# Log-sum-exp of 16384 rows: a range check moved ahead of the last rows, and two bulk loads issued as four transfers each

## The chip, the cores and the metric

The kernel runs on one core of a Trainium2 chip. The metric is device time in microseconds (us) of one execution. Engines: DVE is VectorE, ACT is ScalarE, PE is TensorE, POOL is GpSimd, SP is the engine whose queue issues the loads and the store. "Landing" of a DMA is the moment at which the sixteenth of its sixteen semaphore increments arrives (the trace of the kernel before holds 288 of them for its 18 DMAs).

## The reference

```python
x: float32 [32, 512, 1024]          # np.random.randn
max_x = np.max(x, axis=-1, keepdims=True)
return max_x.squeeze(-1) + np.log(np.sum(np.exp(x - max_x), axis=-1))
```

## The kernel before

The 16384 rows are laid out as 128 partitions with 128 rows (columns of `sumexp`) each. The kernel bets that no row needs its maximum subtracted: it sums exp(x) directly, takes the log, stores the result, and then checks whether every sum lay within a safe range. Only if the check fails does a slow fallback run and overwrite the result. Loads go into a ring of 48 row slots. In the list below `R8` is eight rows whose exp ACT makes and DVE reduces, `T` rows are summed by DVE in another form, and `A` rows by ACT itself.

```python
RING = 48
loads = ["R8 R8", "R8 R8", "R8 R8", "R7 R6 A A", "R6 R5 A A A", "R5 R4 A", "R5 R4", "R5 T3",
         "R3 A A A", "R3 A", "R2 T2", "R3", "R1 A", "T2", "T1", "A", "A"]      # 17 loads, 128 rows
...
def load(p0, c0, size):
    return nc.sync.dma_start(out=ring[:, p0 : p0 + size, :], in_=x_rows[:, c0 : c0 + size, :])
...
    nc.scalar.activation(out=res[:, EARLY:NC], in_=sumexp[:, EARLY:NC], func=AF.Ln)
    nc.sync.dma_start(out=out_view, in_=res)                        # the 18th DMA
    # range check of columns 0..126: clamp, then count what the clamp changed
    nc.vector.tensor_scalar(out=clamped[:, 0:LAST], in0=sumexp[:, 0:LAST], scalar1=LOW, scalar2=HIGH, ...)
    nc.vector.scalar_tensor_tensor(out=clamped[:, 0:LAST], ..., op1=ALU.not_equal, accum_out=bad[:, 0:1])
    nc.tensor.matmul(count, lhsT=bad[:, 0:1], rhs=far, start=True, stop=False)
    # the last row: enough that one of its first 64 inputs is not tiny, and that its sum is not huge
    nc.vector.reduce_max(out=bad[:, 2:3], in_=last_row[:, 0, 0 : d // 16], axis=AX.X)
    nc.vector.tensor_scalar(out=bad[:, 1:2], in0=bad[:, 2:3], scalar1=LOG_LOW, op0=ALU.is_lt, ...)
    nc.tensor.matmul(count, lhsT=bad[:, 1:2], rhs=far, start=False, stop=False)
    nc.tensor.matmul(count, lhsT=sumexp[:, LAST:NC], rhs=ones, start=False, stop=True)
    nc.vector.tensor_scalar(out=fine, in0=count, scalar1=HIGH, op0=ALU.is_lt, ...)
    all_fine = nc.values_load(fine[0:1, 0:1], engines=[ACT, DVE], ...)   # a register on ACT and on DVE
    with tc.If(all_fine < 1):
        ...                                                          # the fallback
```

The framework places all semaphores. DMAs take eight semaphores in rotation (102, 103 and 105 to 110). At the end of the program SP waits for twelve semaphores in a fixed order (105, 106, 103, 107, 102, 108, 113, 109, 112, 110, 101, 104); then SP, ACT, DVE and PE each report with a closing drain, POOL collects the reports (at 162.47 us in the kernel before), and a second closing round follows (POOL has its reports at 162.95).

Of the kernel before, what the change touches and what calls it, by code (L numbers as in the profile page):

```python
# [9 lines left out]
LOW, HIGH = 1e-15, 1e15  # L10
LOG_LOW = -34.0
# [3 lines left out]
def kernel(  # L15
# [5 lines left out]
    nc = tc.nc  # L21
    P = nc.NUM_PARTITIONS
    fp32 = mybir.dt.float32
    i32 = mybir.dt.int32
    AF = mybir.ActivationFunctionType
    AX = mybir.AxisListType
    ALU = mybir.AluOpType

    x_flat = x.flatten_outer_dims()
    n, d = x_flat.shape  # L30
# [4 lines left out]
    x_rows = x_flat.rearrange("(p c) d -> p c d", p=P)  # L35
# [6 lines left out]
    loads = [  # L42
        "R8 R8", "R8 R8", "R8 R8", "R7 R6 A A", "R6 R5 A A A", "R5 R4 A", "R5 R4", "R5 T3",
        "R3 A A A", "R3 A", "R2 T2", "R3", "R1 A", "T2", "T1", "A", "A",
    ]
    loads = [[(op[0], int(op[1:] or 1)) for op in load.split()] for load in loads]
    assert sum(s for ops in loads for _, s in ops) == NC
    ENGINES = [mybir.EngineType.Activation, mybir.EngineType.DVE]
    EARLY = 104
    LAST = NC - 1  # L50

    big = ctx.enter_context(tc.tile_pool(name="big", bufs=1))
    stats = ctx.enter_context(tc.tile_pool(name="stats", bufs=1))
    psum = ctx.enter_context(tc.tile_pool(name="psum", bufs=1, space=bass.MemoryType.PSUM))

    ring = big.tile([P, RING, d], fp32, name="ring")
    sumexp = stats.tile([P, NC], fp32, name="sumexp")
    res = stats.tile([P, NC], fp32, name="res")
    clamped = stats.tile([P, NC], fp32, name="clamped")
    bad = stats.tile([P, 3], fp32, name="bad")  # L60
    fine = stats.tile([1, 1], i32, name="fine")
    far = stats.tile([P, 1], fp32, name="far")
    ones = stats.tile([P, 1], fp32, name="ones")
    last_exp = psum.tile([P, 1, d], fp32, name="last_exp")
    count = psum.tile([1, 1], fp32, name="count")
# [3 lines left out]
    nc.vector.memset(far, 100 * HIGH)  # L69

    def load(p0, c0, size):
        return nc.sync.dma_start(out=ring[:, p0 : p0 + size, :], in_=x_rows[:, c0 : c0 + size, :])  # L72

    def without_wait(ins, group, reason):

        tc.declare_no_dep(ins.ins, group=group, reason=reason)

    c = 0
    p = 0
    for ops in loads:  # L80
        size = sum(s for _, s in ops)
        if p + size > RING:
            p = 0
        dma = load(p, c, size).ins
        for how, s in ops:
            v = ring[:, p : p + s, :]
            sums = sumexp[:, c : c + s]
            if how == "A":
                o = v if c < LAST else last_exp
                exp = nc.scalar.activation(out=o, in_=v, func=AF.Exp, accum_out=sums)  # L90
            else:
                exp = nc.scalar.activation(out=v, in_=v, func=AF.Exp)  # L92
            without_wait(exp, "loads", "the slot's earlier users came before this load")
            without_wait(exp, "exps", "the slot's earlier users came before this load")
            without_wait(exp, "sums", "the slot's earlier users came before this load")
            tc.add_to_no_dep_group("exps", exp.ins)
            added = []
            if how == "R":
                added = [nc.vector.reduce_sum(out=sums, in_=v, axis=AX.X)]  # L99
            elif how == "T":  # L100
                for r in range(s):
                    lo = ring[:, p + r, 0:H]
                    added.append(
                        nc.vector.scalar_tensor_tensor(  # L104
                            out=lo, in0=lo, scalar=1.0, in1=ring[:, p + r, H:d],
                            op0=ALU.mult, op1=ALU.add, accum_out=sums[:, r : r + 1],
                        )
                    )
            for add in added:
                tc.declare_no_dep(add.ins, dma, reason="ScalarE has waited for it")  # L110
                without_wait(add, "loads", "they came before this one")
            for add in added:
                tc.add_to_no_dep_group("sums", add.ins)
            c += s
            p += s
            last_row = v
        tc.add_to_no_dep_group("loads", dma)
        if c == EARLY + 14:
            nc.scalar.activation(out=res[:, 0:EARLY], in_=sumexp[:, 0:EARLY], func=AF.Ln)  # L119

    nc.scalar.activation(out=res[:, EARLY:NC], in_=sumexp[:, EARLY:NC], func=AF.Ln)  # L121
    nc.sync.dma_start(out=out_view, in_=res)




    nc.vector.tensor_scalar(  # L127
        out=clamped[:, 0:LAST], in0=sumexp[:, 0:LAST],
        scalar1=LOW, scalar2=HIGH, op0=ALU.max, op1=ALU.min,
    )  # L130
    nc.vector.scalar_tensor_tensor(  # L131
        out=clamped[:, 0:LAST], in0=clamped[:, 0:LAST], scalar=0.0, in1=sumexp[:, 0:LAST],
        op0=ALU.bypass, op1=ALU.not_equal, accum_out=bad[:, 0:1],
    )
    nc.tensor.matmul(count, lhsT=bad[:, 0:1], rhs=far, start=True, stop=False)  # L135
    nc.vector.reduce_max(out=bad[:, 2:3], in_=last_row[:, 0, 0 : d // 16], axis=AX.X)  # L136
    nc.vector.tensor_scalar(  # L137
        out=bad[:, 1:2], in0=bad[:, 2:3], scalar1=LOG_LOW, scalar2=None, op0=ALU.is_lt
    )
    nc.tensor.matmul(count, lhsT=bad[:, 1:2], rhs=far, start=False, stop=False)  # L140
    nc.tensor.matmul(count, lhsT=sumexp[:, LAST:NC], rhs=ones, start=False, stop=True)  # L141

    nc.vector.tensor_scalar(out=fine, in0=count, scalar1=HIGH, scalar2=None, op0=ALU.is_lt)  # L143
    all_fine = nc.values_load(
        fine[0:1, 0:1], engines=ENGINES, min_val=0, max_val=1,
# [2 lines left out]
    with tc.If(all_fine < 1, preferred_fallthrough_block=False):  # L148
        with tc.tile_critical(sync_engine=mybir.EngineType.Activation):
            with nc.semaphore("landed") as landed, nc.semaphore("ready") as ready:  # L150
                rows = 0
                steps = 0
                for c0 in range(0, NC, RING):
# [3 lines left out]
                    if c0:  # L157
# [5 lines left out]
                        out=neg, in_=v, op=ALU.max, axis=AX.X, negate=True  # L163
# [3 lines left out]
                        out=v, in0=v, in1=neg[:, :, None].to_broadcast([P, s, d])  # L167
# [5 lines left out]
                        out=sumexp[:, c0 : c0 + s], in_=v, axis=AX.X  # L173
# [39 lines left out]
```

## Time and profile before

| | before |
|---|---|
| median (6 runs) | 165.12 us (164.97 to 165.41) |
| traced execution | 164.92 us, span 163.1 us |
| last row lands | 159.01 us |
| store issued, landed | 160.46, 162.01 us |
| SP's and DVE's first closing drain begin | 162.37 and 162.38 us |
| end, counted from the last landing | 4.13 us |

From the page of the kernel before: engine busy time, the data rate in 40 slices, and the DMA queue.

```profile
PE 0.4 (0%) x6; PEld 0.2 (0%) x6; DVE 122.0 (75%) x44; ACT 116.8 (72%) x53; POOL 0.2 (0%) x4
GB/s 257 514 321 450 514 370 402 514 418 354 514 418 354 514 438 407 377 482 482 450 394 422 436 420 402 402 450 434 434 418 442 422 440 400 426 423 421 409 314 18
q1 hardware_dynamic: 2592, 67.18, 95.9%
```

The transfers fill the 16 DMA engines for 95.9% of the span, while DVE (75% busy) and ACT (72%) have slack. The load is the bound. A change that adds no bandwidth can touch only the 1.7 us before the first packet and the last 4 us: what happens after the last row has landed at 159.01.

The timeline of that tail (start, duration, engine, line, operation, output<-input, shapes):

```profile
159.03 1.02 ACT L90 ACTIVATE last_exp<-ring 128x1024 f32<-128x1024 f32 x1
159.29 0.08 DVE L104 DVE_READ_ACCUMULATOR ring<-ring 128x1 f32 x1
159.48 0.23 DVE L127 TENSOR_SCALAR clamped<-sumexp 128x127 f32<-128x127 f32 x1
159.74 0.29 DVE L131 SCALAR_TENSOR_TENSOR clamped<-clamped,sumexp 128x127 f32<-128x127 f32 x1
...
159.96 0.21 DVE L136 TENSOR_REDUCE bad<-ring 128x1 f32<-128x64 f32 x1
160.21 0.15 DVE L137 TENSOR_SCALAR bad<-bad 128x1 f32<-128x1 f32 x1
160.21 0.22 ACT L121 ACTIVATE res<-sumexp 128x24 f32<-128x24 f32 x1
160.46 0.35 SPq L122 DMA_DIRECT2D out_dram<-res  x1
...
160.69 0.14 DVE L143 TENSOR_SCALAR fine<-count 1x1 int32<-1x1 f32 x1 [0.33 <-PE count L141]
```

Two chains start from the last rows. ACT's goes exp, log, store. DVE's goes from its last row sum (line 104) through the range check to `fine`, then a value load and a branch on DVE and ACT. The timeline view leaves out waits and branches, so the records of SP's list and those of DVE and POOL that matter here are printed from the trace itself (those of ACT and PE and some of DVE's are left out): start, duration in ns, engine, instruction, and the semaphores that it waits for. `TENSOR_LOAD` is the value load of `fine`. The store increments semaphore 103.

```
160.86     17 Sync    EVENT_SEMAPHORE   105
160.88    661 Vector  TENSOR_LOAD       (fine)
160.92   1111 Sync    EVENT_SEMAPHORE   106, 103     <- stands here until the store lands at 162.01
161.81     51 Vector  COMPARE_BRANCH
162.06     28 Sync    EVENT_SEMAPHORE   107, 102
162.13     28 Sync    EVENT_SEMAPHORE   108, 113
162.19     28 Sync    EVENT_SEMAPHORE   109, 112
162.25     28 Sync    EVENT_SEMAPHORE   110, 101
162.32      7 Sync    DRAIN             104
162.37      7 Sync    DRAIN             (report to POOL)
162.38     53 Vector  DRAIN             (report to POOL)
162.47     17 GpSimd  EVENT_SEMAPHORE   (all have reported)
```

The view of the waits of SP's queue shows that long wait as a line of its own:

```profile
SPq L208 <- DMA out_dram<-res: 1.1, 1, 1.1
```

After the store has landed, SP still executes four waits, about 0.062 us apart, that have long been satisfied. By chance or by earlier tuning DVE's drain begins within 0.01 us of SP's. It takes 53 ns against SP's 7 and so ends 0.05 us later, at 162.43.

### The profile page before, as it was taken

How to read it: one execution, taken by the hardware profiler on the slowest of the kernel's cores; microseconds unless marked ns; L12 is line 12 of the kernel's file. 1: busy time of each engine (PE TensorE's matmuls, PEld its weight loads, DVE VectorE, ACT ScalarE, POOL GpSimd, SP SyncE). 2: the span in 40 equal slices, each digit the busy share in tenths (PEclk: the TensorE clock that was granted, in tenths of full speed). 3: DMA queues.
4: the chain of work that ended last, by engine and by line, in shares of the span. 5: the costliest groups of instructions: out<-in, count | busy, mean ns of one | idle time of the engine just before them, and what ended most of it. 6: DMA issues, size and time to landing. Idle time of an engine off the chain costs nothing.

```text
span 163.1 us, 198 instructions
## 1 busy us (share of the span) xinstructions
PE 0.4 (0%) x6; PEld 0.2 (0%) x6; DVE 122.0 (75%) x44; ACT 116.8 (72%) x53; POOL 0.2 (0%) x4
## 2 busy tenths in 40 slices
PE   0000000000000000000000000000000000000001
PEld 0000000000000000000000000000000000000000
DVE  0000000699958999499999995999998999979893
ACT  3000039990699708995499829999969599999993
POOL 0000000000000000000000000000000000000000
DMA  6979989998998999899999999999999999999970
GB/s 257 514 321 450 514 370 402 514 418 354 514 418 354 514 438 407 377 482 482 450 394 422 436 420 402 402 450 434 434 418 442 422 440 400 426 423 421 409 314 18
DMA packets 2593, 67.18 MB, mean 412 GB/s; under 512 B 288, under 2 KB 416, under 8 KB 800
## 3 DMA queue, kind: packets, MB, share of 16 engines
q1 hardware_dynamic: 2592, 67.18, 95.9%
q14 instruction: 1, 0.01, 0.0%
HBM read 67.11 MB, written 0.07 MB: 412 GB/s over the span
## 4 chain that ended last, share of the span: by engine, by line
DMA 64%; DVE 22%; ACT 12%; issue 1%; SPq 0%; PE 0%; DVEq 0%
DMA ring<-in_x_dram 64%; DVE sumexp L99 20%; ACT ring L92 12%; DVE ring L104 1%; SPq L72 0%; DVE clamped L127 0%; PE count L140 0%; DVE bad L137 0%; DVE clamped L131 0%; DVE fine L143 0%; DVE bad L136 0%; PE count L141 0%; DVEq L127 0%
## 5 line engine op out<-in xcount | busy, mean ns | idle before, releaser
L99 DVE TENSOR_REDUCE sumexp<-ring 128x8 f32<-128x8192 f32 (+7 forms) x20 | 116.2, 5854 | 37.5 <-ACT ring L92 37.5
L92 ACT ACTIVATE ring<-ring 128x8192 f32<-128x8192 f32 (+7 forms) x24 | 101.7, 4283 | 42.9 <-DMA ring<-in_x_dram 42.9
L90 ACT ACTIVATE ring<-ring 128x1024 f32<-128x1024 f32 x12 | 12.5, 1040 | 0.0
L104 DVE SCALAR_TENSOR_TENSOR ring<-ring 128x512 f32<-128x512 f32 x8 | 5.1, 686 | 0.0
L90 ACT ACTIVATION_READ_ACCUMULATOR ring<-ring 128x1 f32 x12 | 2.2, 186 | 0.0
L67 ACT ACT_TABLE_LOAD x1 | 1.3, 1283 | 0.7 <-PEq L197 0.7
L90 ACT ACTIVATE last_exp<-ring 128x1024 f32<-128x1024 f32 x1 | 1.0, 1024 | 0.0
L104 DVE DVE_READ_ACCUMULATOR ring<-ring 128x1 f32 x8 | 0.7, 83 | 0.0
L68 DVE MEMSET ones<- 128x1 f32 x1 | 0.1, 59 | 0.8 <-PEq L197 0.8
L135 PE MATMUL count<-far,bad 128*1 128x1 f32 x2 | 0.2, 164 | 160.1 <-DVE clamped L131 160.1
L143 DVE TENSOR_SCALAR fine<-count 1x1 int32<-1x1 f32 x1 | 0.1, 145 | 0.3 <-PE count L141 0.3
L131 DVE SCALAR_TENSOR_TENSOR clamped<-clamped,sumexp 128x127 f32<-128x127 f32 x1 | 0.3, 292 | 0.0
L127 DVE TENSOR_SCALAR clamped<-sumexp 128x127 f32<-128x127 f32 x1 | 0.2, 228 | 0.1
L135 PEld LDWEIGHTS count<-far,bad 128*1 128x1 f32 x2 | 0.1, 80 | 160.1 <-DVE clamped L131 160.1
L119 ACT ACTIVATE res<-sumexp 128x104 f32<-128x104 f32 x1 | 0.3, 273 | 0.0
L121 ACT ACTIVATE res<-sumexp 128x24 f32<-128x24 f32 x1 | 0.2, 223 | 0.0
L136 DVE TENSOR_REDUCE bad<-ring 128x1 f32<-128x64 f32 x1 | 0.2, 215 | 0.0
L140 PE MATMUL count<-far,bad 128*1 128x1 f32 x2 | 0.2, 164 | 0.1
L141 PE MATMUL count<-ones,sumexp 128*1 128x1 f32 x2 | 0.2, 163 | 0.0
L90 ACT ACTIVATION_READ_ACCUMULATOR last_exp<-ring 128x1 f32 x1 | 0.2, 186 | 0.0
L137 DVE TENSOR_SCALAR bad<-bad 128x1 f32<-128x1 f32 x1 | 0.2, 153 | 0.0
L141 PEld LDWEIGHTS count<-ones,sumexp 128*1 128x1 f32 x2 | 0.1, 82 | 0.0
(7 smaller groups left out, 0.6 us busy)
## 6 DMA issues: line engine op xcount, KB each, us to landing
ring<-in_x_dram SPq DMA_DIRECT2D x1, 7680.0 KB, 32.4
ring<-in_x_dram SPq DMA_DIRECT2D x1, 7168.0 KB, 30.0
ring<-in_x_dram SPq DMA_DIRECT2D x1, 5120.0 KB, 31.4
ring<-in_x_dram SPq DMA_DIRECT2D x1, 4608.0 KB, 33.7
ring<-in_x_dram SPq DMA_DIRECT2D x1, 4096.0 KB, 29.3
ring<-in_x_dram SPq DMA_DIRECT2D x2, 2048.0 KB, 32.7
ring<-in_x_dram SPq DMA_DIRECT2D x1, 3072.0 KB, 36.3
ring<-in_x_dram SPq DMA_DIRECT2D x2, 1024.0 KB, 38.8
```

The source lines that it names most:

```text
L67: nc.scalar.preload_act_table_set("natural_log_exp_and_others")
L90: exp = nc.scalar.activation(out=o, in_=v, func=AF.Exp, accum_out=sums)
L92: exp = nc.scalar.activation(out=v, in_=v, func=AF.Exp)
L99: added = [nc.vector.reduce_sum(out=sums, in_=v, axis=AX.X)]
L104: nc.vector.scalar_tensor_tensor(out=lo, in0=lo, scalar=1.0, in1=ring[:, p + r, H:d], op0=ALU.mult, op1=ALU.add, accum_out=sums[:, r : r + 1],
L119: nc.scalar.activation(out=res[:, 0:EARLY], in_=sumexp[:, 0:EARLY], func=AF.Ln)
L121: nc.scalar.activation(out=res[:, EARLY:NC], in_=sumexp[:, EARLY:NC], func=AF.Ln)
L127: nc.vector.tensor_scalar(out=clamped[:, 0:LAST], in0=sumexp[:, 0:LAST], scalar1=LOW, scalar2=HIGH, op0=ALU.max, op1=ALU.min,)
L131: nc.vector.scalar_tensor_tensor(out=clamped[:, 0:LAST], in0=clamped[:, 0:LAST], scalar=0.0, in1=sumexp[:, 0:LAST], op0=ALU.bypass, op1=AL ...
L135: nc.tensor.matmul(count, lhsT=bad[:, 0:1], rhs=far, start=True, stop=False)
L136: nc.vector.reduce_max(out=bad[:, 2:3], in_=last_row[:, 0, 0 : d // 16], axis=AX.X)
L141: nc.tensor.matmul(count, lhsT=sumexp[:, LAST:NC], rhs=ones, start=False, stop=True)
```

## The change

The intent: let SP meet the store's semaphore last, so that all other waits are passed while the store is in flight; and shorten the check that is left at the end. For the first, 6 more DMAs are put ahead of the store (24 is a multiple of the 8 semaphores). For the second, the first 118 columns are checked early: the call stands in the program behind the load of rows 118 to 120, with seven rows still to come.

```diff
+    LATE = 118
...
     def load(p0, c0, size):
-        return nc.sync.dma_start(out=ring[:, p0 : p0 + size, :], in_=x_rows[:, c0 : c0 + size, :])
+        step = 4 if c0 in (32, 48) else 1
+        return [
+            nc.sync.dma_start(
+                out=ring[k::step, p0 : p0 + size, :], in_=x_rows[k::step, c0 : c0 + size, :]
+            ).ins
+            for k in range(step)
+        ]
...
+    def check(c0, c1, i):
+        nc.vector.tensor_scalar(out=clamped[:, c0:c1], in0=sumexp[:, c0:c1], ...)
+        nc.vector.scalar_tensor_tensor(out=clamped[:, c0:c1], ..., accum_out=bad[:, i : i + 1])
+        nc.tensor.matmul(count, lhsT=bad[:, i : i + 1], rhs=far, start=i == 0, stop=False)
...
+        if c == LATE + 3:
+            check(0, LATE, 0)
...
-    (the check of columns 0:LAST)
+    check(LATE, LAST, 1)
```

More of the change, by code (lines that the diff above doesn't have):

```diff
@@ L59 @@
     clamped = stats.tile([P, NC], fp32, name="clamped")
-    bad = stats.tile([P, 3], fp32, name="bad")
+    bad = stats.tile([P, 4], fp32, name="bad")
     fine = stats.tile([1, 1], i32, name="fine")
@@ L71, in load @@
     def load(p0, c0, size):
-        return nc.sync.dma_start(out=ring[:, p0 : p0 + size, :], in_=x_rows[:, c0 : c0 + size, :])
+        step = 4 if c0 in (32, 48) else 1
[5 more added lines that the diff above has]
+        ]
     def without_wait(ins, group, reason):
         tc.declare_no_dep(ins.ins, group=group, reason=reason)
+    def check(c0, c1, i):
+        nc.vector.tensor_scalar(
+            out=clamped[:, c0:c1], in0=sumexp[:, c0:c1],
+            scalar1=LOW, scalar2=HIGH, op0=ALU.max, op1=ALU.min,
+        )
+        nc.vector.scalar_tensor_tensor(
+            out=clamped[:, c0:c1], in0=clamped[:, c0:c1], scalar=0.0, in1=sumexp[:, c0:c1],
+            op0=ALU.bypass, op1=ALU.not_equal, accum_out=bad[:, i : i + 1],
+        )
+        nc.tensor.matmul(count, lhsT=bad[:, i : i + 1], rhs=far, start=i == 0, stop=False)
     c = 0
@@ L83 @@
             p = 0
-        dma = load(p, c, size).ins
+        dmas = load(p, c, size)
         for how, s in ops:
@@ L109 @@
             for add in added:
-                tc.declare_no_dep(add.ins, dma, reason="ScalarE has waited for it")
+                for dma in dmas:
+                    tc.declare_no_dep(add.ins, dma, reason="ScalarE has waited for it")
                 without_wait(add, "loads", "they came before this one")
@@ L116 @@
             last_row = v
-        tc.add_to_no_dep_group("loads", dma)
+        for dma in dmas:
+            tc.add_to_no_dep_group("loads", dma)
         if c == EARLY + 14:
             nc.scalar.activation(out=res[:, 0:EARLY], in_=sumexp[:, 0:EARLY], func=AF.Ln)
+        if c == LATE + 3:
+            check(0, LATE, 0)
     nc.scalar.activation(out=res[:, EARLY:NC], in_=sumexp[:, EARLY:NC], func=AF.Ln)
     nc.sync.dma_start(out=out_view, in_=res)
+    check(LATE, LAST, 1)
+    nc.vector.reduce_max(out=bad[:, 3:4], in_=last_row[:, 0, 0 : d // 16], axis=AX.X)
     nc.vector.tensor_scalar(
-        out=clamped[:, 0:LAST], in0=sumexp[:, 0:LAST],
-        scalar1=LOW, scalar2=HIGH, op0=ALU.max, op1=ALU.min,
-    )
-    nc.vector.scalar_tensor_tensor(
-        out=clamped[:, 0:LAST], in0=clamped[:, 0:LAST], scalar=0.0, in1=sumexp[:, 0:LAST],
-        op0=ALU.bypass, op1=ALU.not_equal, accum_out=bad[:, 0:1],
-    )
-    nc.tensor.matmul(count, lhsT=bad[:, 0:1], rhs=far, start=True, stop=False)
-    nc.vector.reduce_max(out=bad[:, 2:3], in_=last_row[:, 0, 0 : d // 16], axis=AX.X)
-    nc.vector.tensor_scalar(
-        out=bad[:, 1:2], in0=bad[:, 2:3], scalar1=LOG_LOW, scalar2=None, op0=ALU.is_lt
-    )
-    nc.tensor.matmul(count, lhsT=bad[:, 1:2], rhs=far, start=False, stop=False)
+        out=bad[:, 2:3], in0=bad[:, 3:4], scalar1=LOG_LOW, scalar2=None, op0=ALU.is_lt
+    )
+    nc.tensor.matmul(count, lhsT=bad[:, 2:3], rhs=far, start=False, stop=False)
     nc.tensor.matmul(count, lhsT=sumexp[:, LAST:NC], rhs=ones, start=False, stop=True)
```

## The prediction

> **What bounds the kernel now.** The input load. The DMA queue table shows 67.18 MB on the hardware queue for 95.9% of 16 engines' span. The trace's packets run back to back on each engine from about 1.7-3.2 us to 158.0-158.6 us (a 64 KB packet starts every 2.42 us, some 434 GB/s over 16 engines). DVE (75%) and ACT (72%) have slack until the last rows. The last row lands at 159.0; only the 4 us after it can be touched.
>
> **The tail** (timeline from 155 us). The last row lands at 159.01. ACT: exp, accumulator, Ln to 160.44; the store is issued at 160.46 and lands at 162.01. From there SP's final waits: it stood 1.11 us at the wait that holds the store's semaphore, the second of its list; then four more wait instructions and a drain, about 0.062 us apart, so its closing drain begins at 162.37. In parallel DVE: last row sums end 159.37, range check 159.48 to 159.96, reduce_max, compare, PE, `fine` at 160.69-0.83, value load, branch, and DVE's closing drain begins at 162.38. So two chains end within 0.01 us of each other, SP's and DVE's; both must shrink for the end to move.
>
> **What the change does.**
> 1. 17 loads become 23, the store is the 24th DMA; with 8 semaphores in rotation it takes the eighth, last in SP's list. The other waits pass while the store is in flight. SP's closing drain moves from 162.37 to about 162.12: -0.25 us.
> 2. The check left at the end works on 9 columns, not 127. By slopes estimated from this trace (0.6 ns per column for the first instruction, 1.0 for the second: 228 ns at 127 columns against 153 at 1; 682 at 512 against 292 at 127), it gets about 0.07 + 0.12 = 0.19 us shorter. `fine` and DVE's drain move 0.19 us earlier. PE is not limiting: the last row's sum is there at 160.19.
> 3. The check of 118 columns costs about 0.5 us of DVE earlier. DVE waits 0.77 us for an exp before 153.06. I expect the scheduler to place the check in that gap (it already hoisted the early Ln), so it is free. If it stands after that reduction instead, DVE, busy without break from 153.06 to 159.37, is pushed back by 0.5 and the end comes about 0.3 us later.
> 4. Six more DMAs. A completion packet delays the next data packet of its engine by only 6 ns: 0.04 us in all. The extra issues (0.33-0.43 us each on SP) fall where tens of us of transfers are queued.
>
> Expected: -0.19 (the slower of the two chains) + 0.04, about -0.15 us of a 165.4 us kernel: 165.2 us, 8-in-10 range 164.7 to 166.0. Faster by over 2%: 0.01; within: 0.93; slower: 0.06.
>
> **What would show it.** Store landing to SP's drain shrinks from 0.36 to about 0.1 us; `fine` at about 160.5; DVE's first check between 152.3 and 153.1; mean GB/s and last landing (159.0) unchanged within 0.2.
>
> **What would make it wrong.** The transfers of 32 partitions at a stride of 4. [...] packets in these two loads (16 MB, 37 us now) take longer than 2.42 us and the whole DMA-bound run is late by 1 us or much more. Worse still: if the framework takes the interleaved quarters for overlapping, they run one after another, with a bubble at each.

## The result, and the profile after

| | before | after |
|---|---|---|
| median of 6 runs | 165.12 us (164.97 to 165.41) | 164.74 us (164.63 to 164.87) |
| ratio, 95% interval | | 0.9975 (0.9962 to 0.9988) |
| last row lands (traced execution) | 159.01 | 159.12 |
| store lands, SP's drain after it | 162.01, +0.36 | 162.11, +0.14 |
| DVE's drain after the last landing | 3.37 | 3.10 |
| end after the last landing | 4.13 | 3.85 |

A ratio is the mean time of one kernel's fast runs over that of the other's of the same rounds, so it is not quite the ratio of the medians. The verdict is "same" at the 2% mark, and a small gain clear of noise. The end relative to the last landing moved by 0.28 us. (Differences are taken before rounding, here and below.)

The same lines of the page, after:

```profile
PE 0.6 (0%) x8; PEld 0.3 (0%) x8; DVE 122.4 (75%) x47; ACT 116.7 (72%) x53; POOL 0.2 (0%) x4
GB/s 257 515 370 402 515 402 370 515 370 402 515 418 354 515 423 377 422 483 483 394 436 394 422 436 402 442 450 434 434 394 450 408 434 416 426 422 420 412 334 20
q1 hardware_dynamic: 2688, 67.18, 96.3%
```

The bound is the same, with the same bytes and 96 packets more (6 DMAs, 16 completion packets each). The timeline, after:

```profile
152.44 0.22 DVE L89 TENSOR_SCALAR clamped<-sumexp 128x118 f32<-128x118 f32 x1
152.70 0.28 DVE L93 SCALAR_TENSOR_TENSOR clamped<-clamped,sumexp 128x118 f32<-128x118 f32 x1
...
153.17 4.48 DVE L120 TENSOR_REDUCE sumexp<-ring 128x3 f32<-128x3072 f32 x2 [0.18 <-ACT ring L113]
...
159.16 1.01 ACT L111 ACTIVATE last_exp<-ring 128x1024 f32<-128x1024 f32 x1
159.40 0.08 DVE L125 DVE_READ_ACCUMULATOR ring<-ring 128x1 f32 x1
159.59 0.17 DVE L89 TENSOR_SCALAR clamped<-sumexp 128x9 f32<-128x9 f32 x1
159.80 0.17 DVE L93 SCALAR_TENSOR_TENSOR clamped<-clamped,sumexp 128x9 f32<-128x9 f32 x1
...
159.91 0.22 DVE L152 TENSOR_REDUCE bad<-ring 128x1 f32<-128x64 f32 x1
160.32 0.22 ACT L146 ACTIVATE res<-sumexp 128x24 f32<-128x24 f32 x1
160.57 0.35 SPq L147 DMA_DIRECT2D out_dram<-res  x1
160.65 0.14 DVE L158 TENSOR_SCALAR fine<-count 1x1 int32<-1x1 f32 x1 [0.33 <-PE count L157]
```

The first check stands in the gap in which DVE waited for ACT before 153.17, although the program calls it behind that reduction: the framework's scheduler moved it there; of that idle time (0.77 us before) 0.18 is left, and the reduction behind it still starts as soon as ACT releases it. At the end, the time from the check's first instruction to the reduction behind it fell from 0.48 to 0.32 us. The rest of the tail, from the trace's records as above; the store now increments semaphore 110:

```
160.83    542 Vector  TENSOR_LOAD       (fine)
160.97     17 Sync    EVENT_SEMAPHORE   105
161.02     28 Sync    EVENT_SEMAPHORE   106, 103
161.08     28 Sync    EVENT_SEMAPHORE   107, 102
161.15    453 Sync    EVENT_SEMAPHORE   108, 113     <- DVE, behind its value load
161.63    244 Sync    EVENT_SEMAPHORE   109, 112     <- ACT, behind its value load
162.12     28 Sync    EVENT_SEMAPHORE   110, 101     <- the store, landed at 162.11
162.19      7 Sync    DRAIN             104
162.21     50 Vector  DRAIN             (report to POOL)
162.24      7 Sync    DRAIN             (report to POOL)
162.30     17 GpSimd  EVENT_SEMAPHORE   (all have reported)
```

In the view of SP's waits, one wait of 1.1 us has become several that end in order, with the store's as the last and only 0.2 us long:

```profile
SPq L223 <- DVEq L163: 0.5, 1, 0.5
SPq L223 <- ACTq L163: 0.3, 1, 0.3
SPq L223 <- DMA out_dram<-res: 0.2, 1, 0.2
```

The two closing drains begin within 0.03 us of each other again, both about a quarter of a microsecond earlier. They end at 162.25 (SP) and 162.26 (DVE).

### The profile page after: what moved, and what is told of

The parts are those of the page before. It is cut to its first block, busy times and chain, and to the rows that moved or that the text cites. A ratio compares the mean times of both kernels' runs of the same rounds, so it can differ in the third digit from the quotient of the medians.

```text
span 163.0 us, 216 instructions
## 1 busy us (share of the span) xinstructions
PE 0.6 (0%) x8; PEld 0.3 (0%) x8; DVE 122.4 (75%) x47; ACT 116.7 (72%) x53; POOL 0.2 (0%) x4
## 4 chain that ended last, share of the span: by engine, by line
DMA 64%; DVE 22%; ACT 12%; issue 0%; SPq 0%; PE 0%; DVEq 0%
DMA ring<-in_x_dram 64%; DVE sumexp L120 21%; ACT ring L113 12%; DVE ring L125 1%; SPq L77 0%; PE count L156 0%; DVE clamped L89 0%; DVE bad L153 0%; DVE bad L152 0%; DVE clamped L93 0%; DVE fine L158 0%; PE count L157 0%; DVEq L89 0%
## 5 line engine op out<-in xcount | busy, mean ns | idle before, releaser
L93 DVE SCALAR_TENSOR_TENSOR clamped<-clamped,sumexp 128x118 f32<-128x118 f32 (+1 forms) x2 | 0.5, 225 | 0.1
```

The lines of the kernel that those rows point to most:

```text
L93: nc.vector.scalar_tensor_tensor(out=clamped[:, c0:c1], in0=clamped[:, c0:c1], scalar=0.0, in1=sumexp[:, c0:c1], op0=ALU.bypass, op1=ALU.n ...
```

## The experiments

The theory: two chains end together, SP's waits behind the store and DVE's check with its branch. The end is the later of the two, so each half of the change alone is worth almost nothing, and both together are worth about what the lesser gains. The rivals: one half carries all of the gain; or the split itself does something in the load phase.

All results in one table, the times in us. "SP" is SP's closing drain counted from the landing of the store, "DVE" is DVE's closing drain and "end" the end of the program, both counted from the last landing.

| kernel | median | before, same rounds | ratio (95%) | last landing | SP | DVE | end |
|---|---|---|---|---|---|---|---|
| before | 165.12 | | | 159.01 | 0.36 | 3.37 | 4.13 |
| before again (e11) | 165.11 | 165.15 | 0.9993 (0.9979 to 1.0006) | 159.18 | 0.36 | 3.38 | 4.13 |
| the change | 164.74 | 165.12 | 0.9975 (0.9962 to 0.9988) | 159.12 | 0.14 | 3.10 | 3.85 |
| again (e6) | 164.78 | 165.29 | 0.9966 (0.9951 to 0.9981) | 159.18 | 0.14 | 3.07 | 3.83 |
| a third time (e12) | 164.74 | 165.02 | 0.9979 (0.9965 to 0.9992) | 159.20 | 0.14 | 3.08 | 3.84 |
| e1 split only | 165.28 | 165.28 | 1.0003 (0.9990 to 1.0017) | 159.23 | 0.14 | 3.38 | 4.13 |
| e2 check only | 165.14 | 165.28 | 0.9998 (0.9985 to 1.0012) | 159.30 | 0.36 | 3.09 | 4.06 |
| e3 check behind the reduction | 165.52 | 165.28 | 1.0013 (0.9999 to 1.0026) | 159.41 | 0.39 | 3.57 | 4.32 |
| e4 first two loads split | 165.34 | 165.28 | 1.0006 (0.9992 to 1.0019) | 159.79 | 0.14 | 3.20 | 3.95 |
| e5 split in blocks | 206.74 | 165.29 | 1.2509 (1.2485 to 1.2533) | 200.89 | 0.14 | 3.11 | 3.86 |
| e7 no check | 165.12 | 165.29 | 0.9988 (0.9972 to 1.0003) | 159.30 | 0.14 | none | 4.03 |
| e8 one load split | 165.17 | 165.29 | 0.9993 (0.9976 to 1.0010) | 159.24 | 0.32 | 3.10 | 4.04 |
| e9 split by rows | 165.25 | 165.15 | 1.0002 (0.9988 to 1.0017) | 159.65 | 0.14 | 3.07 | 3.83 |
| e10 two queues | 165.29 | 165.15 | 1.0001 (0.9987 to 1.0016) | 159.68 | 0.14 | 3.06 | 3.84 |

e1 to e4 ran on one chip, e5 to e8 on another, e9 to e11 on a third, e12 on a fourth.

### e1: the split alone

```diff
-        if c == LATE + 3:
-            check(0, LATE, 0)
...
-    check(LATE, LAST, 1)
+    check(0, LAST, 0)
```

> Only the eight transfers and the shifted semaphore; the whole range check stays at the end, as before. Two-chain theory: SP's closing drain comes about 0.12 us after the store lands (0.36 before), but DVE still reaches its closing drain near 162.4 us, so the end hardly moves: ratio to before 0.9990 to 1.0010. Rival (the semaphore order alone carries the gain): ratio about 0.9975, as the whole change had.

SP is ready 0.14 us after the store, as with the change. DVE is not: its drain comes 3.38 us after the last landing, and the end stays at 4.13. The records:

```
162.36      7 Sync    DRAIN             (report to POOL; the store landed at 162.22)
162.61     51 Vector  DRAIN             (report to POOL; the last row landed at 159.23)
162.69     17 GpSimd  EVENT_SEMAPHORE   (all have reported)
```

The semaphore order alone is worth nothing, and the rival falls.

### e2: the check alone

```diff
-        step = 4 if c0 in (32, 48) else 1
+        step = 1
```

> Only the check moved; the loads and the semaphore of the store as before. Two-chain theory: the last compare (fine) ends about 0.2 us earlier counted from the last landing and DVE's closing drain comes near 162.2, but SP still passes its waits one by one for 0.36 us after the store lands, so the end stays: ratio 0.9990 to 1.0005. Rival (the shorter check alone carries the gain): ratio about 0.9975.

DVE is early (3.09), SP late (0.36). SP's view shows the long wait of before again:

```profile
SPq L223 <- DMA out_dram<-res: 1.1, 1, 1.1
```

The end moves by 0.07 us only. It moves at all because in the kernel before POOL had waited for the end of DVE's drain, at 162.43 us, 0.05 us after that of SP's at 162.38. So the gains 0.00 and 0.07 of the halves do not add up to the 0.28 of the whole: the signature of two chains that end together.

### e3: the first check behind a busy stretch of DVE

```diff
-    LATE = 118
+    LATE = 121
-        if c == LATE + 3:
+        if c == LATE:
```

> As the change, but the first check covers 121 columns and so has to stand behind the reduction of rows 118 to 120, where DVE is busy without a break. Theory: DVE's work up to the last row sums is pushed back by about 0.45 us and the end by about 0.3 us against the change (the second check is 3 columns narrower, which is worth under 0.01): ratio to before 0.9990 to 1.0010. Rival (DVE has slack at the end, or its chain does not decide): ratio 0.9975, as the change.

The timeline of this kernel shows the check without a gap before it, and the row sums pushed back:

```profile
153.47 4.48 DVE L120 TENSOR_REDUCE sumexp<-ring 128x3 f32<-128x3072 f32 x2 [0.77 <-ACT ring L113]
157.87 0.21 DVE L89 TENSOR_SCALAR clamped<-sumexp 128x121 f32<-128x121 f32 x1
158.12 0.29 DVE L93 SCALAR_TENSOR_TENSOR clamped<-clamped,sumexp 128x121 f32<-128x121 f32 x1
158.33 0.69 DVE L125 SCALAR_TENSOR_TENSOR ring<-ring 128x512 f32<-128x512 f32 x1
```

The 0.77 us gap before the reduction is back and unused, and the next row sum starts 0.46 us after the check's first instruction. DVE's drain and the end both come 0.47 us later than with the change (expected: 0.3), and the ratio of 1.0013 lies just above the range expected. The whole push of 0.46 us arrives at the end; I had expected a third of it to be lost. SP's drain is late too (0.39), although the store's semaphore stands last: its list also holds waits for DVE and ACT behind their value loads, and here the later of these is passed 0.24 us after the store has landed. The placement of the early check is therefore what makes it free, and three columns' difference in where it may start decides it.

### e4: the first two loads split instead, to start the engines sooner

```diff
-        step = 4 if c0 in (32, 48) else 1
+        step = 4 if c0 in (0, 16) else 1
```

> As the change, but the first two loads are the ones issued as four transfers each, so the store has the same semaphore. In the trace of before the 16 engines start their first packet between 1.73 and 3.23 us. Theory: [...] a first transfer of 32 descriptors lets all engines start by about 2.2 us, so the last landing is 0.3 to 0.9 us earlier: ratio to before 0.992 to 0.996. Rival (the stagger has nothing to do with the size of the first transfer): start and end as with the change, ratio about 0.9975.

The expectation failed: the ratio is 1.0006. The first packet starts at 2.05 us, not 1.75, the engines' first packets are spread over 1.73 us (0.86 with the change), and the last landing comes 0.67 us later. The spread should not be read too closely: in before, whose first two loads are the same as those of the change, it is 1.50 us, and in e6, the change's second trace, 1.39 us. The trace's records show about half of the delay of the first packet: SP takes 0.54 us to issue the first quarter, and 0.57 to 0.83 for the next, against 0.38 and 0.42 for the full 128-partition loads in the change. A transfer of every fourth partition is not quicker to issue but slower. It is the stride that costs and not the size, as e5 shows: its blocks of 32 adjacent partitions take 0.31 to 0.42 us. The fourth transfer on SP's queue, where it follows the first three at once, is an exception whatever its shape: 0.83 us here, 0.78 in the change, 0.89 in e5 and 1.01 in e9, where it has 128 partitions; in all eleven such traces it takes 0.76 to 1.01 us. In the change the same cost is paid at 1.6 to 4.2 us and 47 to 50 us, where earlier transfers keep the engines busy (0.98 of their time from 42 to 61 us), and is hidden. The tail is 0.10 us longer than the change's as well: from the check's first instruction to the reduction behind it DVE takes 0.41 us here, against 0.30 to 0.32 in the nine other traces with the short check. What causes this, the spread of the first packets and the rest of the later landing stays open.

### e5: blocks of 32 partitions instead of every fourth

```diff
+        n = 32 if c0 in (32, 48) else P
-                out=ring[k::step, p0 : p0 + size, :], in_=x_rows[k::step, c0 : c0 + size, :]
-            for k in range(step)
+                out=ring[k : k + n, p0 : p0 + size, :], in_=x_rows[k : k + n, c0 : c0 + size, :]
+            for k in range(0, P, n)
```

> As the change, but the four transfers of the two loads take partitions 0 to 31, 32 to 63, 64 to 95 and 96 to 127 instead of every fourth partition. Theory: [...] the 16 MB of these two loads, 37.5 us now, take up to twice that and the 61440 and 65536 byte packets in them up to twice 2.3 and 2.4 us: time 10 to 38 us longer, ratio 1.06 to 1.23. Rival (any split in four is as good): ratio 0.9975 and packets as now.

The data rate in 40 slices of this kernel's 204.8 us:

```profile
GB/s 307 474 435 422 410 410 410 410 294 205 205 205 218 205 205 198 240 228 192 204 192 192 192 314 403 437 408 440 448 404 418 435 442 416 423 419 427 415 399 27
```

From about 43 to 120 us, while these two loads run, the rate is half (mostly 192 to 240 GB/s, against 400 to 448 after it), and the 61440-byte packets take 4.79 us (median) instead of 2.27. That is a factor of 2.11, where I had expected up to two; no trace here shows why blocks are slow. Time rose by 41 us, slightly more than my upper bound. The stride of 4 in the change is not a matter of taste. With it the packets in the two loads keep their medians of 2.42 and 2.27 us, and the two loads land 19.35 and 18.15 us after the load before each, to the hundredth as in the kernel before. In the trace of the change the first load's quarters land one after another, at 47.22, 52.07, 56.88 and 61.72 us. The strided split gains no bandwidth here, but it costs none either.

### e6: the change once more

> The change itself once more, to stand beside the others on one chip. From the trace of the first run the end comes 3.85 us after the last landing (4.12 before); ratio 0.9970 to 0.9990.

The end again comes 3.83 us after the last landing. The ratio, 0.9966, is just below the range that I gave: see e11 and e12.

### e7: neither check nor fallback (right for this data only)

```diff
-        if c == LATE + 3:
-            check(0, LATE, 0)
...
-    check(LATE, LAST, 1)
-    ...                       # all up to the end of the fallback
```

> The change without range check and fallback (right for this data only; it measures what the check still costs). Two-chain theory: with the change both chains end together again, so taking DVE's away leaves SP's: end 3.80 to 3.86 us after the last landing, ratio 0.9965 to 0.9980, hardly better than the change. Rival (DVE's and ACT's branch is still the later one by far): end 3.6 us or less after the last landing, ratio below 0.9960.

Neither expectation held for the end: 4.03 us, worse than with the check. The first closing round is as the theory has it: SP's drain comes 0.14 us after the store and POOL's gate, the moment at which it has all reports, 0.17 us after it (0.17 to 0.19 in the change's three traces), so the remaining check costs at most 0.02 us in that round. But in the second closing round ACT's drain starts at 162.98, 0.3 us after SP's and DVE's (162.68 and 162.71), and holds up all. In the change ACT, SP and DVE start theirs within 0.03 us. Without the branch ACT's program is another, and something delays it there; what it is this run does not show. "SP's chain is the floor" is supported by the first round alone.

### e8: one load split, the store on the fifth semaphore of eight

```diff
-        step = 4 if c0 in (32, 48) else 1
+        step = 4 if c0 == 32 else 1
```

> As the change, but only one of the two loads is split, so there are 20 loads and the store takes the fifth semaphore of the rotation, which is in the middle of SP's list. Theory: after the landing of the store SP has three more wait instructions of about 0.062 us than with the change, so its closing drain comes 0.29 to 0.33 us after the landing (0.13 with the change, 0.36 before) and the end about 4.0 us after the last landing: ratio 0.9980 to 0.9995. Rival (the split itself, not the place of the semaphore, makes the difference): SP's closing drain 0.13 us or 0.36 us after the landing of the store.

SP's drain comes 0.32 us after the store, with three further waits behind the one that holds it, against 0.14 with none and 0.36 with four. The end is at 4.04, 0.19 later than with the change: 3 x 0.062. Only the position of the store's semaphore in SP's list counts, not how often a load was split.

### e9 and e10: the six DMAs by cutting rows, and a second queue

```diff
-        "R8 R8", "R8 R8", "R8 R8", "R7 R6 A A", "R6 R5 A A A", "R5 R4 A", "R5 R4", "R5 T3",
+        "R8", "R8", "R8", "R8", "R8", "R8", "R7", "R6 A A", "R6", "R5 A A A", "R5", "R4 A", "R5 R4", "R5 T3",
-        step = 4 if c0 in (32, 48) else 1
+        step = 1
```

> As the change, but the six more loads come from cutting six loads in two by rows, all of 128 partitions; no transfer is cut by partitions. The store is again the 24th DMA. Theory (only the number of DMAs ahead of the store counts): SP's closing drain 0.13 us after the landing of the store, end 3.85 us after the last landing, ratio 0.9965 to 0.9980, as the change. Rival (the stride over partitions does something of its own, good or bad): ratio off the change's by more than 0.0015.

The tail is that of the change (3.83), but the ratio is not (1.0002): the last landing comes half a microsecond later and eats the gain. The packets tell why: cut by rows, a 65536-byte packet becomes two of 32768, and two of these take 2 x 1.213 = 2.426 us against 2.420; altogether there are 2944 data packets instead of 2176. Median durations times counts, over 16 engines, come to 155.97 us against 155.54: 0.43 us of the 0.53 (159.65 against 159.12). Cutting by every fourth partition, as the change does, leaves the packets as they are (medians of 2.42 and 2.27 us). So the rival had a point: how the loads are cut matters, though not in the tail.

e10 adds to e9 that the second load is issued from ACT's queue at the same moment as the first. For that the preload of ACT's tables, which the cut below leaves out, is moved behind that load:

```diff
-            nc.sync.dma_start(
+            (nc.scalar if c0 == 8 else nc.sync).dma_start(
```

> As the row split, but the second load (rows 8 to 15) is issued on ACT's queue at the same moment as the first on SP's; an attempt to beat both kernels. If the spread of the engines' first packets (1.73 to 2.6 us or more in all traces so far) comes from SP feeding one engine after another, all engines start by about 2.2 us and the last landing comes 0.2 to 0.5 us earlier: ratio 0.994 to 0.996. Rival (the spread does not come from the queue): as the row split, 0.9965 to 0.9980.

The engines' first packets still spread from 1.74 to 2.74 us (1.75 to 2.61 in e9): the second queue did not narrow the spread, and what sets it is not shown. The last landing, at 159.68 us, is about that of e9 (159.65). The attempt to beat both kernels failed.

### e11 and e12: before and the change once more

> The kernel before once more, for a second trace of it: the traced execution of before was the fastest of its runs (164.92 us; median about 165.25). The two chains account for 0.27 us of the 0.4 to 0.5 us by which the change's median is lower. If the rest lies in the load phase, this trace, if its time is near the median, has its last landing at 159.25 to 159.4 us (159.01 in the first trace) and the end again 4.13 us after it. Rival (the tail varies): landing near 159.0 to 159.15 and a tail of 4.3 us or more. Ratio 0.999 to 1.001.

> The change a third time. Its 12 runs so far lie between 164.63 and 164.87 us, while before and every variant with the same tail as before scatter over 0.3 to 0.8 us, and its medians are 0.38 and 0.51 us under those of before, of which the tail explains 0.28. If the rest is the luck of the load phase in those executions, the runs now scatter more and the ratio comes to 0.9975 to 0.9990; if it belongs to the change, they lie again within 0.3 us and the ratio is 0.9965 to 0.9978. The tail is 3.83 to 3.86 us in either case.

These two were to settle a remainder. On the first two occasions the medians differed by 0.38 and 0.51 us, and the tail explains 0.28. The second trace of before (165.09 us) has a tail of 4.13 again and its last landing at 159.18, a little earlier than I expected, and no later than in the change's traces (159.12, 159.18 and 159.20). On the third occasion the medians differ by 0.28 us, what the tail explains. The change's medians hardly moved over the three (164.74, 164.78, 164.74), those of before did (165.12, 165.29, 165.02). The tail's 0.28 us is a ratio of 0.9983; it lies inside the intervals of the first and third occasion and just outside that of the second. So the remainder came and went with the runs of before. I ascribe it to the load phase, where e1 (159.23), e3 (159.41) and the change (159.12), which issue the same loads in the same order, differ by up to 0.29 us in one trace each. But no trace shows one of the slow runs of before (165.4 us and above), so that stays argued and not shown. The change's 17 runs scatter little (164.62 to 164.97); why they do is open.

## Why the prediction was right, and where its terms were off

The prediction was right: 164.74 us lies inside 164.7 to 166.0, with "within 2%" the outcome. But it lies 0.04 us from the edge, and that is partly luck: the prediction started from 165.4 us, where the kernel before measured 165.12 in these rounds, and the gain was 0.38 us by the medians and 0.28 in the tail, where 0.15 was predicted. The mechanism was right, and the size of DVE's term was not (point 3). Point by point:

1. *The load is the bound, only the tail can move*: right. The data rate and the medians of the packets did not change.
2. *SP's closing drain 0.25 us earlier*: measured 0.36 to 0.14 after the landing of the store, 0.23. e8 confirms the mechanism in between.
3. *The check at the end 0.19 us shorter*: the check itself is shorter by 0.16 (0.48 to 0.32). But DVE's drain moved by 0.28 against the last landing. The missing 0.12 is DVE's value load: 661 and 668 ns in the two traces of before and 677 in e1, but 536 to 558 in all ten traces with the short check. I had taken its duration as given. Why it is shorter is not shown. This is the term that was mis-sized: with it both chains gain about a quarter of a microsecond, so that the lesser gain is 0.23 and not 0.19. The end moved by DVE's 0.28, a little more than SP's gain, because DVE's drain was the last to end both before (by 0.05 us) and after (by 0.01).
4. *The first check placed in DVE's gap, free*: right, and e3 shows what the other placement costs: 0.47 us against the change. Against the kernel before it ends 0.20 us later (4.32 against 4.13); the prediction had said 0.3 for this case.
5. *Six more DMAs cost 0.04 us*: not visible. The next data packet follows 6 ns (median, in both traces) after a completion packet has started, and the loads that were split land 19.35 and 18.15 us after their predecessors in both kernels. Of the 0.11 us by which the last row landed later in the first trace, 0.10 was there when the second load landed (42.37 against 42.27), before any split transfer had landed. What the prediction missed is that issuing a strided quarter takes SP 0.47 to 0.61 us (0.78 for the fourth transfer of the program), not 0.33 to 0.43; it is hidden here, and e4 shows the case where it isn't.
6. *Packets in the split loads might take longer than 2.42 us*: with the stride of 4 they did not (medians of 2.42 and 2.27 us, as before), and no bubble shows: both loads took as long as in the kernel before (19.35 and 18.15 us). In blocks (e5) the 61440-byte packets took 4.79 us instead of 2.27; why blocks differ is not shown.

The sum predicted was 0.15 us; the tail gave 0.28. The difference is the 0.04 that cost nothing, and the two chains' gains (0.23 and 0.28, not 0.25 and 0.19). What put the medians up to 0.51 us apart on top of that is not shown.

## What to carry to other kernels

When a program ends with several engines reporting to a barrier, find every chain that ends there; if two end together, a change to one of them is worth almost nothing (0.00 and 0.07 us here), and it takes both halves to see the gain. In a fixed list of final waits, the one that is satisfied last should stand last: each wait behind it costs about 0.06 us here. If a load must be cut in pieces, cut it so that packets keep their size and their duration (every fourth partition did here, blocks of 32 did not), keep the pieces away from the start (in e4 the last row landed 0.67 us later), and put extra vector work where the trace shows the engine waiting (it was free in the gap of 0.77 us, and cost 0.47 us behind it).
